# The second softmax's factor of a differential attention on GpSimd instead of VectorE, with other waits in its written order

## The chip, the core and the metric

The kernel runs on one core of one Trainium2 chip. The metric is device time in microseconds (us) of one execution, the median of three runs. The core's engines work side by side, each through its own queue in order: TensorE (PE, matmuls and transposes), VectorE (DVE), ScalarE (ACT), GpSimd (POOL) and SyncE (SP, which issues the DMA transfers). Semaphores hold an instruction until its inputs are there.

## What is computed

One layer of an encoder over 512 tokens of width 1024, all in float32: a norm, one input projection, three branches (pooling, differential attention, a gated recurrence), their gated sum, an output projection, and a SwiGLU block. The change touches the attention, four heads, 128 queries at a time. Of the reference:

```python
s = jnp.einsum('bqhcd,bkhcd->bhcqk', qblk, k) * scale
s = s - slopes[:, None, None, None] * dist
p = jax.nn.softmax(s, axis=-1)
a = (p[:, :, 0] - lam * p[:, :, 1]).astype(v.dtype)
return jnp.einsum('bhqk,bkhe->bqhe', a, v)
...
o = rms_norm(o, gain) * (1.0 - lambda_init)
```

Each head has two softmaxes (c = 0 and 1). With e0, e1 the exponentials and z0, z1 their row sums, the kernel makes e0 + co * e1 with co = -lam * z0 / z1, which is z0 times the wanted difference; the head's norm brings 1/z0 in later.

## The kernel before

The program is one long list of TensorE work in an order written by hand. `Pipe.run` (L45) takes several generators, called streams here, and resumes the first whose time has come: `mm` and `transpose` add an assumed duration to a clock of its own, `yield ("w", t)` lets a stream sit out t of that clock, and `yield ("e", name, t)` makes it wait for a marked event and t more. `mm` and `transpose` keep TensorE's instructions in just that order (`keep_in_program_order`). No such yield becomes an instruction; it only decides what stands between two pieces of one stream. On the other engines a scheduler in the compiler orders the instructions.

In the attention stage run together: `att_head(h)` for four heads, `pool_windows()` (running sums for the pooling branch, VectorE alone) and `jobs.stream` (the projections: per job eight 128x512 matmuls each of `hT_hi` with `whi`, `hT_lo` with `whi`, `hT_hi` with `wlo`; the branch projections read `y_arena` instead). Each job's weights arrive by DMA in `raw`; ScalarE rounds them into `whi` (L183) and VectorE subtracts the rest into `wlo` (L184). Weight buffers are three deep, so a later `wlo` waits for TensorE to finish an earlier job.

`att_front_job` makes a head's operands: q from one job, k from the next. Of k, ScalarE makes two rounded copies (L1019, L1020), VectorE the rest `l` (L1021) and ScalarE a copy of that (L1023), for c = 0 and then for c = 1.

`att_head(h)`, four query blocks i of 128 rows each:

- `scores(i)`: for c = 0, 1 two 128x512 matmuls into a bank of `rc` (q with k, q with l); VectorE adds the distance penalty and takes the row's minimum (L1056, `s` and `mx`); ScalarE takes the exponential and its row sum into `zz` (L1058, an activation and a short read of its accumulator). Then on VectorE: reciprocals of both row sums (L1062, `rr`), the factor `co` (L1064), and the combination over 128x512 (L1066, `s`).
- `turn(i)`: TensorE transposes that `s` in four pieces into `tp` (L98); ScalarE rounds it into `aT_hi` (L1075), VectorE subtracts into `aT_lo` (L1076).
- after four blocks, twelve matmuls `rc<-aT,va` with the values, then `head_norm`: squares on ScalarE, their sums by matmuls with `onesD`, three small VectorE operations `mo` (L663 to L665) that bring in 1/z0, a power of -0.5 on GpSimd (L140, `rso`), one more product on VectorE (L667) and transposes of `rso`.

Blocks are named head.block below, 0.0 to 3.3. A block's combination must be done when its transposes come up in TensorE's queue, or all matmuls behind them wait. Two lines of the loop set the distance:

```python
yield ("w", 1.8 + (0.7 if i == 0 else 0.0))   # L1080, then scores(i + 1)
yield ("w", 1.6 + (1.0 if i + h == 0 else 0.0))   # L1085, then turn(i)
```

Of the kernel before, what the change touches and what calls it, by code (L numbers as in the profile page):

```python
# [11 lines left out]
F32 = mybir.dt.float32  # L12
# [3 lines left out]
ALU = mybir.AluOpType  # L16
PSUM = bass.MemoryType.PSUM

P = 128
S = 512  # L20
D = 1024
NB = S // P
# [16 lines left out]
class Pipe:  # L39
# [8 lines left out]
    def mark(self, name):  # L48
        self.events[name] = self.t
# [27 lines left out]
def encoder_kernel(ctx: ExitStack, tc: tile.TileContext, x, norm1_g, w_in, pool_w, pool_scale,  # L77
# [3 lines left out]
    nc = tc.nc  # L81
# [3 lines left out]
    def pool(name, bufs=1, **kw):  # L85
        return tc.tile_pool(name=name, bufs=bufs, **kw)


    def mm(out_, lhsT, rhs, start, stop, chain=False):
        i = nc.tensor.matmul(out_, lhsT=lhsT, rhs=rhs, start=start, stop=stop, skip_group_check=chain)  # L90
        tc.keep_in_program_order(i)
        n = 1
        for d in rhs.shape[1:]:
            n *= d
        pipe.t += max(0.107, n * 0.0004167 + 0.002) if rhs.dtype == F32R else max(0.216, n * 0.001667 + 0.004)

    def transpose(out_, in_, idn):
        tc.keep_in_program_order(nc.tensor.transpose(out_, in_, idn))  # L98
        pipe.t += 0.108
# [8 lines left out]
    const = ctx.enter_context(pool("const"))  # L108
    wraw = ctx.enter_context(pool("wraw", 2))
    wsp = ctx.enter_context(pool("wsp", 3))  # L110
    small = ctx.enter_context(pool("small", 5))
    psum = ctx.enter_context(pool("psum", 3, space=PSUM))

    def bank(name, shape=(P, 512)):
        return psum.tile(list(shape), F32, name=name, bufs=2 if name == "tp" else 3)
# [11 lines left out]
    nc.vector.memset(onesD, 1.0 / P)  # L127
    mhalf = const.tile([P, 8], F32, name="mhalf")
    nc.vector.memset(mhalf, -0.5)
    masks = const.tile([P, len(LEVELS), P], U8, name="masks")  # L130
    vcol = const.tile([P, 14], F32, name="vcol")
    gain_a = const.tile([P, 1], F32, name="gain_a")
    lb = const.tile([P, 8], F32, name="lb")
    om = const.tile([P, 8], F32, name="om")
    nlam = const.tile([P, 1], F32, name="nlam")
# [3 lines left out]
    def pow_mhalf(dst, src):  # L139
        return nc.gpsimd.tensor_tensor(out=dst, in0=src, in1=mhalf[:, :src.shape[1]], op=ALU.pow).ins  # L140

    def rsqrt_eps(dst, mean):

        ms = small.tile([P, 8], F32, name="ms")[:, :mean.shape[1]]
        eng = nc.vector if mean.space == PSUM else nc.gpsimd
        eng.tensor_scalar(out=ms, in0=mean, scalar1=1.0, scalar2=EPS, op0=ALU.mult, op1=ALU.add)
        return pow_mhalf(dst, ms)
# [431 lines left out]
    ps = bank("mm")  # L579
# [67 lines left out]
    def head_norm(o_ps, tmp, gain, r0=None, bufs=2):  # L647


        og = tmp.tile([P, S], F32, name="og", bufs=bufs)  # L650
        sq = tmp.tile([P, S], F32, name="sqo", bufs=bufs)
        nc.scalar.activation(out=sq, in_=o_ps, func=AF.Square)
        nc.scalar.activation(out=og, in_=o_ps, func=AF.Copy, scale=gain)
        yield ("w", 1.3)
        sp = bank("tp")
        for b in range(NB):
            mm(sp[:, b:b + 1], sq[:, b * P:(b + 1) * P], onesD, True, True)
        r = small.tile([P, NB], F32, name="rso")
        if r0 is None:
            rsqrt_eps(r, sp[:, 0:NB])  # L660
        else:
            m = small.tile([P, NB], F32, name="mo")
            nc.vector.tensor_tensor(out=m, in0=sp[:, 0:NB], in1=r0, op=ALU.mult)  # L663
            nc.vector.tensor_tensor(out=m, in0=m, in1=r0, op=ALU.mult)
            nc.vector.tensor_scalar(out=m, in0=m, scalar1=EPS, scalar2=None, op0=ALU.add)  # L665
            pow_mhalf(r, m)
            nc.vector.tensor_tensor(out=r, in0=r, in1=r0, op=ALU.mult)  # L667
        yield ("w", 3.55)
        rb = bank("tp")
        for b in range(NB):  # L670
            transpose(rb[:, b * P:(b + 1) * P], r[:, b:b + 1].to_broadcast([P, P]), ident)
        return og, rb
# [359 lines left out]
    def att_head(h):  # L1032
        if h:
            yield ("e", f"QK{h - 1}", 0.0)
        if h > 1:
            yield ("e", f"AN{h - 2}", 0.0)
        yield ("e", f"AF{h}", 6.0)
        t = att.pop(h)
        at, (vh, vl), aT, y_attn = ATT["at"], ATT["v"], ATT["aT"], ATT["y"]
        strip = ATT["strip"].tile([P, 896], F32, name="strip")  # L1040
        nc.sync.dma_start(out=strip, in_=c_dist[h])
        zz = at.tile([P, NB, 2], F32, name="zz")
        rr = at.tile([P, NB, 2], F32, name="rr")
        probs = {}

        def scores(i):
            bs = slice(i * P, (i + 1) * P)
            mx = small.tile([P, 2], F32, name="mx")
            ex = []
            for c in range(2):  # L1050
                ps = bank("rc")
                mm(ps, t[f"q{c}"][:, bs], t[f"k{c}"], True, False)
                mm(ps, t[f"q{c}"][:, bs], t[f"l{c}"], False, True)
                s = at.tile([P, S], F32, name=f"s{c}")

                nc.vector.tensor_tensor_reduce(out=s, in0=strip[:, 384 - P * i:896 - P * i], in1=ps, scale=1.0,  # L1056
                                               scalar=3.0e38, op0=ALU.add, op1=ALU.min, accum_out=mx[:, c:c + 1])
                nc.scalar.activation(out=s, in_=s, func=AF.Exp, scale=-1.0, bias=mx[:, c:c + 1],  # L1058
                                     accum_out=zz[:, i, c:c + 1])
                ex.append(s)  # L1060

            nc.vector.reciprocal(out=rr[:, i, :], in_=zz[:, i, :])  # L1062
            co = small.tile([P, 1], F32, name="co")
            nc.vector.scalar_tensor_tensor(out=co, in0=zz[:, i, 0:1], scalar=nlam, in1=rr[:, i, 1:2],  # L1064
                                           op0=ALU.mult, op1=ALU.mult)
            nc.vector.scalar_tensor_tensor(out=ex[0], in0=ex[1], scalar=co, in1=ex[0], op0=ALU.mult, op1=ALU.add)  # L1066
            probs[i] = ex[0]

        def turn(i):
            bs = slice(i * P, (i + 1) * P)  # L1070
            p = probs.pop(i)
            pt = bank("tp", (P, NB, P))
            for k in range(NB):
                transpose(pt[:, k, :], p[:, k * P:(k + 1) * P], ident)
            nc.scalar.copy(out=aT[0][:, :, bs], in_=pt)  # L1075
            nc.vector.tensor_tensor(out=aT[1][:, :, bs], in0=pt, in1=aT[0][:, :, bs].bitcast(F32), op=ALU.subtract)  # L1076

        scores(0)
        for i in range(NB):
            yield ("w", 1.8 + (0.7 if i == 0 else 0.0))  # L1080
            if i + 1 < NB:
                scores(i + 1)
            else:
                mark(f"QK{h}")
            yield ("w", 1.6 + (1.0 if i + h == 0 else 0.0))  # L1085
            if h and i == 0:
                yield ("e", f"PV{h - 1}", 0.0)
            turn(i)
        mark(f"T{h}")
        yield ("e", "VA", 1.5)  # L1090
        yield ("w", 1.5)
        ps = bank("rc")
        es = slice(h * P, (h + 1) * P)
        terms = [(vh, aT[0]), (vl, aT[0]), (vh, aT[1])]
        for i, (a, r) in enumerate(terms):
            for k in range(NB):
                mm(ps, a[:, k, es], r[:, k, :], i == 0 and k == 0, i == 2 and k == NB - 1)
            yield
        mark(f"PV{h}")
        og, rbp = yield from head_norm(ps, at, gain_a, rr[:, :, 0], 1)  # L1100
        mark(f"AN{h}")
        nc.vector.tensor_tensor(out=og, in0=og, in1=rbp, op=ALU.mult)
        nc.scalar.copy(out=y_attn[0][:, h, :], in_=og)
        nc.vector.tensor_tensor(out=y_attn[1][:, h, :], in0=og, in1=y_attn[0][:, h, :].bitcast(F32),
                                op=ALU.subtract)
# [725 lines left out]
```

## Time and profile before

| what | value |
|---|---|
| median of three runs | 886.88 us (886.32 to 886.91) |
| the profiled execution's own time | 886.27 us |
| its span, first to last instruction | 884.5 us |
| TensorE busy (matmuls) | 867.9 us, 98% |
| VectorE busy | 664.5 us, 75% |
| ScalarE busy | 448.4 us, 51% |
| GpSimd busy | 18.7 us, 2%, 35 instructions |
| attention stage | about 215 to 345 us of the span |

A timeline row has the start in us from the span's start, the duration in us, engine, line, operation, the tile written and the tiles read, the count, and in brackets the idle time before it with what ended it. A matmul row's duration runs into the next one's start, since matmuls overlap; the step from start to start is what TensorE spends. In a row of the waits stand: who waited, for whom, us in total, times, the longest.

### The profile page before, as it was taken

How to read it: one execution, taken by the hardware profiler on the slowest of the kernel's cores; microseconds unless marked ns; L12 is line 12 of the kernel's file. 1: busy time of each engine (PE TensorE's matmuls, PEld its weight loads, DVE VectorE, ACT ScalarE, POOL GpSimd, SP SyncE). 2: the span in 40 equal slices, each digit the busy share in tenths (PEclk: the TensorE clock that was granted, in tenths of full speed). 3: DMA queues.
4: the chain of work that ended last, by engine and by line, in shares of the span. 5: the costliest groups of instructions: out<-in, count | busy, mean ns of one | idle time of the engine just before them, and what ended most of it. 6: DMA issues, size and time to landing. Idle time of an engine off the chain costs nothing.

```text
span 884.5 us, 14079 instructions
## 1 busy us (share of the span) xinstructions
PE 867.9 (98%) x5713; PEld 786.7 (89%) x5713; DVE 664.5 (75%) x1005; ACT 448.4 (51%) x718; POOL 18.7 (2%) x35
## 2 busy tenths in 40 slices
PE   8999999999999989999999999999999999999996
PEld 7989988888998867899999898999999999988885
DVE  6788664844857876987877555998888888747996
ACT  6544343434746743553455334755555655533463
POOL 1000000000000000000000001000000000000001
PEclk9999999999999999999999999999999999999999
DMA  8330113024123311334331770153443443355002
GB/s 243 96 120 24 49 48 116 27 73 141 49 88 94 94 61 49 96 96 137 101 97 48 262 191 1 49 143 96 125 115 96 123 118 97 119 190 189 2 1 96
DMA packets 115693, 87.53 MB, mean 99 GB/s; under 512 B 3862, under 2 KB 104748, under 8 KB 115628
## 3 DMA queue, kind: packets, MB, share of 16 engines
q1 hardware_dynamic: 115036, 85.57, 32.0%
q8 instruction: 45, 0.74, 0.3%
q10 hardware_dynamic: 592, 1.05, 0.3%
q14 instruction: 20, 0.16, 0.1%
HBM read 84.52 MB, written 2.10 MB: 98 GB/s over the span
## 4 chain that ended last, share of the span: by engine, by line
PE 87%; DVE 7%; DMA 2%; issue 1%; ACT 1%; POOL 0%; SPq 0%; POOLq 0%; DVEq 0%; ACTq 0%
PE mm L90 58%; PE rc L90 26%; PE tp L90 2%; PE tp L98 1%; DVE wlo L184 1%; DMA raw<-in_w_out_dram 1%; DMA raw<-in_w_in_dram 1%; DVE hid L354 1%; DVE flo L354 1%; DMA xin<-in_x_dram 0%; DVE s L1066 0%; DVE win L1159 0%; DVE hrow L481 0%; DVE h_lo L498 0%; PE rc L98 0%
## 5 line engine op out<-in xcount | busy, mean ns | idle before, releaser
L183 ACT CAST whi<-raw 128x1024 fp32r<-128x1024 f32 (+1 forms) x134 | 127.5, 958 | 138.4 <-PE mm L90 88.6
L184 DVE TENSOR_TENSOR wlo<-raw,whi 128x1024 fp32r<-128x1024 f32 (+1 forms) x134 | 147.6, 1106 | 58.2 <-ACT whi L183 35.5
L90 PE MATMUL mm<-hT_hi,whi 128*128 128x512 f32 (+1 forms) x344 | 82.1, 371 | 0.0
L90 PE MATMUL mm<-hT_hi,wlo 128*128 128x512 f32 (+1 forms) x344 | 81.7, 370 | 0.2 <-DVE wlo L184 0.2
L90 PE MATMUL mm<-hT_lo,whi 128*128 128x512 f32 (+1 forms) x344 | 81.5, 372 | 0.0
L302 DVE TENSOR_TENSOR slo<-sums,shi 128x1024 fp32r<-128x1024 f32 x58 | 70.5, 1218 | 0.2 <-ACT shi L300 0.2
L90 PEld LDWEIGHTS mm<-hT_lo,whi 128*128 128x128 f32 x344 | 60.0, 191 | 9.9
L90 PEld LDWEIGHTS mm<-hT_hi,whi 128*128 128x128 f32 x344 | 58.9, 189 | 9.9 <-ACT hT_hi L494 0.4
L90 PEld LDWEIGHTS mm<-hT_hi,wlo 128*128 128x128 f32 x344 | 58.5, 188 | 9.5 <-DVE wlo L184 0.4
L300 ACT CAST shi<-sums 128x1024 fp32r<-128x1024 f32 x58 | 61.0, 1053 | 4.1 <-DVE sums L264 3.7
L261 DVE TENSOR_TENSOR sums<-raw 128x1024 f32<-128x1024 f32 x29 | 35.4, 1219 | 1.7 <-DMA raw<-in_w_in_dram 1.6
L90 PE MATMUL mm<-y_arena,whi 128*128 128x512 f32 x128 | 32.8, 394 | 0.0
L90 PE MATMUL mm<-whi,y_arena 128*128 128x256 f32 (+1 forms) x192 | 31.9, 315 | 0.4 <-ACT whi L183 0.2
L914 DVE TENSOR_TENSOR kq<-kq,pyr 128x256 f32<-128x256 f32 x48 | 18.2, 421 | 18.2 <-PE rc L90 18.2
L90 PE MATMUL rc<-kq,kc 128*128 128x128 f32 x224 | 31.6, 284 | 0.0
L90 PEld LDWEIGHTS rc<-kq,kc 128*128 128x128 f32 x224 | 30.1, 191 | 1.5
L1058 ACT ACTIVATE s<-s,mx 128x512 f32<-128x512 f32 x32 | 23.0, 720 | 16.7 <-DVE mx L1056 16.5
L90 PEld LDWEIGHTS mm<-whi,y_arena 128*128 128x128 f32 x192 | 27.4, 188 | 3.5 <-ACT whi L183 1.0
L883 ACT COPY kc<-kq 128x512 f32<-128x512 f32 x28 | 18.6, 666 | 20.2 <-PE rc L90 12.6
L90 PEld LDWEIGHTS mm<-y_arena,whi 128*128 128x128 f32 x128 | 23.7, 188 | 5.1
L1346 DVE TENSOR_TENSOR g<-mm,g 128x256 f32<-128x256 f32 x21 | 8.9, 424 | 23.7 <-PE mm L90 23.7
L90 PE MATMUL mm<-fhi,slo 128*128 128x256 f32 x168 | 26.1, 277 | 0.5 <-DVE slo L302 0.5
(383 smaller groups left out, 2031.5 us busy)
## 6 DMA issues: line engine op xcount, KB each, us to landing
raw<-in_w_in_dram SPq DMA_DIRECT2D x44, 512.0 KB, 4.2
raw<-in_w_ffn_in_dram SPq DMA_DIRECT2D x44, 512.0 KB, 5.3
raw<-in_w_in_dram SPq DMA_DIRECT2D x8, 1024.0 KB, 5.2
raw<-in_w_ffn_out_dram SPq DMA_DIRECT2D x7, 1024.0 KB, 5.0
raw<-in_w_out_dram SPq DMA_DIRECT2D x4, 1024.0 KB, 11.1
xin<-in_x_dram SPq DMA_DIRECT2D x4, 512.0 KB, 4.6
raw<-in_w_up_rec_dram SPq DMA_DIRECT2D x2, 1024.0 KB, 6.4
raw<-in_w_up_pool_dram SPq DMA_DIRECT2D x2, 1024.0 KB, 5.1
```

The source lines that it names most:

```text
L90: i = nc.tensor.matmul(out_, lhsT=lhsT, rhs=rhs, start=start, stop=stop, skip_group_check=chain)
L98: tc.keep_in_program_order(nc.tensor.transpose(out_, in_, idn))
L183: nc.scalar.copy(out=hi, in_=view)
L184: LAST["wlo"] = nc.vector.tensor_tensor(out=lo, in0=view, in1=hi.bitcast(F32), op=ALU.subtract).ins
L261: nc.vector.tensor_tensor(out=strided(sums, 0, [[2 * half, 2], [1, half]]), in0=strided(self.raw, 0, [[3 * half, 2], [1, half]]), in1=stri ...
L300: nc.scalar.copy(out=hi, in_=view)
L302: on_dve = nc.vector.tensor_tensor(out=lo, in0=view, in1=hi.bitcast(F32), op=ALU.subtract).ins
L354: last[0] = form(**kw).ins
L883: nc.scalar.copy(out=strided(kc, 0, [[2 * n, S // (2 * n)], [n, 2], [1, n]]), in_=strided(kq, 2 * S, [[2 * n, S // (2 * n)], [S + n, 2], [ ...
L914: nc.vector.tensor_tensor(out=xv, in0=xv, in1=tv, op=ALU.mult)
L1058: nc.scalar.activation(out=s, in_=s, func=AF.Exp, scale=-1.0, bias=mx[:, c:c + 1], accum_out=zz[:, i, c:c + 1])
L1346: on_dve = nc.vector.tensor_tensor(out=c["g"], in0=c["x"], in1=c["g"], op=ALU.add).ins
```

## The change

The factor leaves VectorE. Per block GpSimd makes `zn` = z0 * -lam, `co` = z1 to the power of -1 (with a column of -1.0, `minus1`), and `co` = `co` * `zn`; the combination on VectorE is as it was, now waiting for GpSimd. The reciprocal of z0 is taken once per head for all four blocks, behind the last `turn`. The yield ahead of `scores(i + 1)` goes from 1.8 to 1.6, the one ahead of `turn(i)` from 1.6 to 2.4. One memset of 128x1 is new at the start. Lines move down by two or three.

```diff
+    minus1 = const.tile([P, 1], F32, name="minus1")
+    nc.vector.memset(minus1, -1.0)
...
-        rr = at.tile([P, NB, 2], F32, name="rr")
+        rr = at.tile([P, NB], F32, name="rr")
...
-            nc.vector.reciprocal(out=rr[:, i, :], in_=zz[:, i, :])
-            co = small.tile([P, 1], F32, name="co")
-            nc.vector.scalar_tensor_tensor(out=co, in0=zz[:, i, 0:1], scalar=nlam, in1=rr[:, i, 1:2],
-                                           op0=ALU.mult, op1=ALU.mult)
+            zn, co = (small.tile([P, 1], F32, name=n) for n in ("zn", "co"))
+            nc.gpsimd.tensor_tensor(out=zn, in0=zz[:, i, 0:1], in1=nlam, op=ALU.mult)
+            nc.gpsimd.tensor_tensor(out=co, in0=zz[:, i, 1:2], in1=minus1, op=ALU.pow)
+            nc.gpsimd.tensor_tensor(out=co, in0=co, in1=zn, op=ALU.mult)
             nc.vector.scalar_tensor_tensor(out=ex[0], in0=ex[1], scalar=co, in1=ex[0], op0=ALU.mult, op1=ALU.add)
...
         for i in range(NB):
-            yield ("w", 1.8 + (0.7 if i == 0 else 0.0))
+            yield ("w", 1.6 + (0.7 if i == 0 else 0.0))
             if i + 1 < NB:
                 scores(i + 1)
             else:
                 mark(f"QK{h}")
-            yield ("w", 1.6 + (1.0 if i + h == 0 else 0.0))
+            yield ("w", 2.4 + (1.0 if i + h == 0 else 0.0))
             if h and i == 0:
                 yield ("e", f"PV{h - 1}", 0.0)
             turn(i)
         mark(f"T{h}")
+        nc.vector.reciprocal(out=rr, in_=zz[:, :, 0])
...
-        og, rbp = yield from head_norm(ps, at, gain_a, rr[:, :, 0], 1)
+        og, rbp = yield from head_norm(ps, at, gain_a, rr, 1)
```

TensorE, from the last score matmul of block 3.3 to its transposes; `s_3066` and `s_3103` are block 3.2, `s_3125` and `s_3168` block 3.3. Before:

```order
L90 MATMUL rc<-l_2760,q_2756 128x512
L90 MATMUL mm<-y_arena,whi 128x512 x2
L90 MATMUL mm<-y_arena,wlo 128x512 x4
L90 MATMUL mm<-y_arena,whi 128x512 x2
L98 MATMUL tp<-ident,s_3066 128x128 x4
L90 MATMUL mm<-y_arena,whi 128x512 x6
L90 MATMUL mm<-y_arena,wlo 128x512 x4
L90 MATMUL mm<-hT_hi,whi 128x512 x8
L98 MATMUL tp<-ident,s_3125 128x128 x4
```

And of the change:

```order
L90 MATMUL rc<-l_2765,q_2761 128x512
L90 MATMUL mm<-y_arena,whi 128x512 x8
L90 MATMUL mm<-y_arena,wlo 128x512 x4
L98 MATMUL tp<-ident,s_3103 128x128 x4
L90 MATMUL mm<-hT_hi,whi 128x512 x8
L90 MATMUL mm<-hT_lo,whi 128x512 x8
L90 MATMUL mm<-hT_hi,wlo 128x512 x4
L98 MATMUL tp<-ident,s_3168 128x128 x4
```

Between the last score matmul and the transposes stood 26 other matmuls of 128x512, now 32, and one block's transposes both times.

VectorE at the same place, behind the two minima of block 3.3. Before, from the first row behind them; behind these twelve follow `co`, `pwlo`, the `gate` combination of L1168 and then the combination of block 3.3:

```order
L1181 TENSOR_TENSOR dlo<-gate,dhi 128x512
L756 TENSOR_TENSOR merged<-mm,gate 128x512
L1159 TENSOR_TENSOR win<-win 128x525
L1076 TENSOR_TENSOR aT_lo<-tp,aT_hi 128x4x128
L1130 MEMSET gate 128x8
L1131 MEMSET gate 128x8
L1062 RECIPROCAL rr<-zz 128x2
L1130 MEMSET gate 128x8
L1131 MEMSET gate 128x8
L756 TENSOR_TENSOR merged<-mm,gate 128x512
L1166 SCALAR_TENSOR_TENSOR win<-win,rcnt 128x2x8
L184 TENSOR_TENSOR wlo<-raw,whi 128x1024
```

Of the change, from the second memset behind the minima up to the combination:

```order
L1134 MEMSET gate 128x8
L1184 TENSOR_TENSOR dlo<-gate,dhi 128x512
L1169 SCALAR_TENSOR_TENSOR win<-win,rcnt 128x2x8
L1092 RECIPROCAL rr<-zz 128x4
L758 TENSOR_TENSOR merged<-mm,gate 128x512
L1133 MEMSET gate 128x8
L1134 MEMSET gate 128x8
L1171 SCALAR_TENSOR_TENSOR gate<-win,gate 128x512
L186 TENSOR_TENSOR wlo<-raw,whi 128x1024
L1178 TENSOR_TENSOR pwlo<-pw,pwhi 128x512
L1078 TENSOR_TENSOR aT_lo<-tp,aT_hi 128x4x128
L1068 SCALAR_TENSOR_TENSOR s_3168<-s_3174,co,s_3168 128x512
```

One `merged`, one `win` of 128x525 and `co` no longer stand between the minima and the combination; the first two now stand ahead of the minima.

TensorE at the first scores of head 2, from the end of the job that makes its k (`mm<-hT_hi,wlo`). Before:

```order
L90 MATMUL mm<-hT_hi,wlo 128x512 x2
L90 MATMUL mm<-y_arena,whi 128x512 x8
L90 MATMUL mm<-y_arena,wlo 128x512 x4
L90 MATMUL mm<-y_arena,whi 128x512 x4
L98 MATMUL tp<-ident,s_2632 128x128 x4
L90 MATMUL mm<-y_arena,whi 128x512 x4
L90 MATMUL mm<-y_arena,wlo 128x512 x4
L90 MATMUL rc<-aT_hi,va_hi 128x512 x4
L90 MATMUL rc<-aT_hi,va_lo 128x512 x4
L90 MATMUL rc<-aT_lo,va_hi 128x512 x4
L90 MATMUL rc<-k_2506,q_2504 128x512
```

And of the change:

```order
L90 MATMUL mm<-hT_hi,wlo 128x512 x8
L90 MATMUL mm<-y_arena,whi 128x512 x4
L98 MATMUL tp<-ident,s_2588 128x128 x4
L90 MATMUL mm<-y_arena,whi 128x512 x4
L90 MATMUL mm<-y_arena,wlo 128x512 x4
L90 MATMUL mm<-y_arena,whi 128x512 x8
L90 MATMUL mm<-y_arena,wlo 128x512 x4
L98 MATMUL tp<-ident,s_2651 128x128 x4
L90 MATMUL rc<-k_2521,q_2519 128x512
L90 MATMUL rc<-l_2523,q_2519 128x512
L90 MATMUL rc<-k_2522,q_2520 128x512
L90 MATMUL rc<-l_2524,q_2520 128x512
```

The first scores of head 2 now stand ahead of head 1's product with the values, and 24 matmuls of 128x512 and two blocks' transposes behind the end of the k job, where 36 matmuls and one block's transposes stood.

## The prediction

> **What bounds the kernel now.** First the page: busy time per engine, then the waits of TensorE.
>
> ```profile
> PE 867.9 (98%) x5713; PEld 786.7 (89%) x5713; DVE 664.5 (75%) x1005; ACT 448.4 (51%) x718; POOL 18.7 (2%) x35
> ```
>
> ```profile
> PE tp L98 <- DVE s L1066: 2.8, 1, 2.8
> PE tp L98 <- DVE rr L1062: 1.0, 1, 1.0
> PE tp L98 <- DVE rso L667: 0.6, 1, 0.6
> ```
>
> TensorE is busy in 98% of the span, and its list of matmuls is the same before and after. So VectorE time taken off is worth nothing in itself: the time moves only where TensorE stands still or runs at a lower clock. These three waits, all in the attention stage, are most of what a change there can win. Now TensorE's timeline at them, with one undisturbed job as the measure.
>
> ```profile
> 340.69 1.99 PE L90 MATMUL mm<-hT_lo,whi 128*128 128x512 f32 x8
> 342.52 0.61 PE L90 MATMUL mm<-hT_hi,wlo 128*128 128x512 f32 x2
> 343.69 0.62 PE L98 MATMUL tp<-ident,rso 128*128 128x128 f32 x4 [0.56 <-DVE rso L667]
> ...
> 276.42 1.08 PE L90 MATMUL mm<-y_arena,wlo 128*128 128x512 f32 x4
> 277.65 1.20 PE L90 MATMUL rc<-aT_hi,va_hi 128*128 128x512 f32 x4
> ...
> 309.30 0.95 PE L90 MATMUL tp<-onesD,sqo 128*128 128x1 f32 x8
> 311.25 0.63 PE L98 MATMUL tp<-ident,s 128*128 128x128 f32 x4 [1.01 <-DVE rr L1062]
> ...
> 320.18 0.39 PE L90 MATMUL rc<-l,q 128*128 128x512 f32 x1
> ...
> 324.98 1.98 PE L90 MATMUL mm<-hT_hi,whi 128*128 128x512 f32 x8
> 329.75 1.09 PE L98 MATMUL tp<-ident,s 128*128 128x128 f32 x4 [2.79 <-DVE s L1066]
> 330.49 3.06 PE L90 MATMUL mm<-hT_lo,whi 128*128 128x512 f32 x8
> 333.39 1.08 PE L90 MATMUL rc<-aT_hi,va_hi 128*128 128x512 f32 x4
> ```
>
> Eight matmuls step 342.52 - 340.69 = 1.83 us, 0.229 each; I count losses from start to start. Block 3.3: 329.75 - 324.98 - 1.83 = 2.94. Block 3.0: the eight passes of `onesD` step about 0.81 elsewhere in this stage, so 311.25 - 309.30 - 0.81 = 1.14. The norm of head 3: 343.69 - 342.52 - 2 x 0.229 = 0.71. The product with the values of head 1: 277.65 - 276.42 - 4 x 0.229 = 0.31. Behind the longest wait the work itself is slow: the eight matmuls at 330.49 take 2.90 instead of 1.83, the transposes 0.74 instead of 0.35, 1.46 lost. The windows say why.
>
> ```profile
> 328.00:330.00 2.00, 0.25 (x2) 0.28 (x3) 1.60 (x3) 0.00 (x0) 0.00 (x0) 0.79 0.00 0
> 330.00:332.00 2.00, 2.00 (x8) 1.71 (x8) 0.51 (x1) 0.59 (x1) 0.00 (x0) 0.50 0.00 0
> ```
>
> The granted clock (third number from the end) falls to 0.50 in the 2.8 us wait. Together 2.94 + 1.14 + 0.71 + 0.31 + 1.46 = **6.56 us** are there to be won, no more.
>
> **Part 1: the factor on GpSimd.** What goes from VectorE and what the new operations cost:
>
> ```profile
> 287.08 0.17 DVE L1062 RECIPROCAL rr<-zz 128x2 f32<-128x2 f32 x1 [0.91 <-ACT s L1058]
> 287.28 0.22 DVE L1064 SCALAR_TENSOR_TENSOR co<-zz,nlam,rr 128x1 f32<-128x1 f32 x1
> 287.54 0.75 DVE L1066 SCALAR_TENSOR_TENSOR s<-s,co,s 128x512 f32<-128x512 f32 x1
> ```
>
> ```profile
> L140 POOL TENSOR_TENSOR rstd<-ms,mhalf x8: 550/554/562, 6.0 to 553.2; 128x1 f32<-128x1 f32 x8
> L146 POOL TENSOR_SCALAR ms<-ss x8: 192/192/419, 5.7 to 552.9; 128x1 f32<-128x1 f32 x8
> ```
>
> From the second row sum (the releaser in the first row, 0.03 ahead of it) to the combination VectorE needs 287.54 - 287.08 + 0.03 = 0.49 us. On GpSimd `zn` needs only z0 and is early. Then comes a power of 128x1, 0.55 by the row above (exponent -0.5 there, -1 here), and a product of 128x1, for which the nearest row is `ms`, 0.19. With some 0.08 at each of three handovers that is 0.98 us, 0.5 longer. VectorE loses 16 x (0.17 + 0.22 + gaps of 0.05) = 7.0 us and gains 4 reciprocals of 0.17 per run; both lie beside TensorE's work. What counts is whether the combination, first in VectorE's queue while GpSimd works, holds what stands behind it: at most 0.5 us per block if nothing else is late.
>
> GpSimd can be held itself:
>
> ```profile
> 283.96 0.75 DVE L1066 SCALAR_TENSOR_TENSOR s<-s,co,s 128x512 f32<-128x512 f32 x1
> 284.18 1.40 POOL L140 TENSOR_TENSOR rso<-mo,mhalf 128x4 f32<-128x4 f32 x1 [20.22 <-DVE mo L665]
> ...
> 200.06 1.01 POOL L140 TENSOR_TENSOR rso<-ms,mhalf 128x4 f32<-128x4 f32 x1 [52.81 <-DVE ms L146]
> 200.92 1.23 DVE L184 TENSOR_TENSOR wlo<-raw,whi 128x1024 fp32r<-128x1024 f32 x1 [0.94 <-PE mm L90]
> ```
>
> A power that began during a combination took 1.40 instead of the 1.01 of the third row, longer by about what was left of that combination. The other way round, a `wlo` that began 0.15 before a power ended took its usual 1.23. So a GpSimd operation may wait out a `wlo` (1.2 us), but then VectorE is at work, not idle; the cost left over is again about one power and one product. I take 0.5 us of need per block, bounds 0 and 0.5 + 1.2. The Trainium skill, page "SBUF — State Buffer", section "Who interferes with whom", speaks against the change: a VectorE instruction with two inputs in SBUF and a GpSimd instruction that reads SBUF lock each other out, and whichever comes second waits for the whole of the first. By that rule VectorE's combinations and `wlo` would wait for powers too, and up to 16 x 0.93 = 15 us of VectorE time would be added, an estimate from the rows above; the trace agrees for GpSimd waiting (1.40) and not for VectorE waiting (1.23).
>
> **Part 2: the distances.** The order rows above give TensorE's work from the start of a block's last score matmul to its transposes; transposes of an earlier block cost about 0.46 with the step behind them.
>
> Block 3.3: before 27 x 0.229 + 0.46 = 6.6 us, after 33 x 0.229 + 0.46 = 8.0.
>
> ```profile
> 318.31 1.23 DVE L184 TENSOR_TENSOR wlo<-raw,whi 128x1024 fp32r<-128x1024 f32 x1
> ...
> 321.94 0.68 DVE L1056 CUSTOM_DVE_ANT_0 s<-strip,rc 128x512 f32<-128x512 f32 x1
> ...
> 323.76 0.68 DVE L756 TENSOR_TENSOR merged<-mm,gate 128x512 f32<-128x512 f32 x1
> 324.36 0.70 DVE L1159 TENSOR_TENSOR win<-win 128x525 f32<-128x525 f32 x1
> ...
> 328.86 0.75 DVE L1066 SCALAR_TENSOR_TENSOR s<-s,co,s 128x512 f32<-128x512 f32 x1
> ```
>
> The need before was 329.60 - 320.18 = 9.4: VectorE has no idle time before any row from the `wlo` to the combination, and eleven pieces of other work lay between the minima and the combination. Now one `merged` and one `win` (0.6 each by their steps) and `co` (0.2) are gone from there, 1.4 less. Both stand ahead of the minima instead, but the first `wlo` row, which starts as the matmuls before it end, now has 12 matmuls and a block's transposes between it and the scores instead of 6, 1.8 us more, against 1.2 us of added rows: the minima come 0.6 sooner. Need 9.4 - 1.4 - 0.6 = 7.4 to 9.4, against 8.0: a stall of 0 to 1.4; I take 0.3, near the lower end, because the rows removed are counted and only the start is unsure.
>
> Block 3.0:
>
> ```profile
> 304.43 0.39 PE L90 MATMUL rc<-l,q 128*128 128x512 f32 x1
> ```
>
> ```profile
> 310.36 0.74 DVE L1066 SCALAR_TENSOR_TENSOR s<-s,co,s 128x512 f32<-128x512 f32 x1
> ```
>
> Need 310.36 + 0.74 - 304.43 = 6.7; offered 5.7 before, and after 27 matmuls and `onesD`, 27 x 0.229 + 0.81 = 7.0. The wait of 1.14 goes. All other blocks gain 0.7 to 1.9 us of distance against 0.5 of need, but for 1.0 and 1.1, which had over 12 us of slack; the tightest of the rest, 1.3, had its combination done 0.5 us early and gets 1.3 more.
>
> The norm of head 3 now has 12 matmuls instead of 18 between `onesD` and its transposes, 2.7 us for a chain that took 4.8; but two `win` additions, the `gate` combination and a `wlo`, which stood among or ahead of its small steps, now come before or after all of them, and what is left (0.5 on VectorE, 1.0 to 1.6 on GpSimd, 0.2) fits. 0.71 goes; bounds 0 and 0.71.
>
> **What is new and late.** Head 2's scores come earlier against the job that makes its k: 24 matmuls and two transposes, 6.4 us to the first, 7.1 to the last that needs the second `l`. The two chains of this kind in the trace:
>
> ```profile
> 271.38 2.01 PE L90 MATMUL mm<-y_arena,whi 128*128 128x512 f32 x8
> ...
> 297.34 0.62 PE L90 MATMUL mm<-hT_hi,whi 128*128 128x512 f32 x2
> ```
>
> ```profile
> 278.56 0.62 ACT L1023 CAST l<-l 64x512 fp32r<-64x512 f32 x1
> ...
> 303.14 0.62 ACT L1023 CAST l<-l 64x512 fp32r<-64x512 f32 x1
> ```
>
> The jobs end where these matmul rows begin; the second `l` was ready 279.18 - 271.38 = 7.8 and 303.76 - 297.34 = 6.4 us later. Against 7.1 that is a stall of 0.7 or none; I take 0.4. For head 3 the distance stays 7.1.
>
> **The sum.** 886.27 (the profiled execution; span 884.5 and 1.8 around it) - 6.56 + 0.3 + 0.4 = 880.4. The median of the runs is 0.6 above that execution: **881.0 us**. The extra memset and the 48 small GpSimd instructions have idle queues.
>
> **Rivals.**
> 1. The last block still waits. VectorE's burst is shifted, not shortened: need near 9.4, stall 1.4, and the clock falls again, 1.46. That gives 881.0 - 0.3 + 2.9 = 883.6. For it: VectorE had no pause there. Against: three rows are gone. A wait of 1.0 us at block 3.0 cost no clock.
> 2. The win is given back behind the stage. VectorE is fully busy there:
>
> ```profile
> 350.00:360.00 10.00, 10.00 (x46) 8.24 (x45) 10.00 (x12) 6.64 (x9) 0.00 (x0) 1.00 0.00 0
> ```
>
> TensorE arrives 6 us sooner, VectorE owes the same sums, and a later `wlo` is late: up to 6.56 back, 886.9. The change would then do what it says and not show. Against: VectorE waits for TensorE itself before that stretch:
>
> ```profile
> 338.22 1.22 DVE L184 TENSOR_TENSOR wlo<-raw,whi 128x1024 fp32r<-128x1024 f32 x1 [6.04 <-PE mm L90]
> ```
>
> 3. Slower. In the burst of blocks 3.1 to 3.3 each combination waits for a power held by a `wlo` (1.2) and a product held by a `win` (0.6): 0.98 + 1.2 + 0.6 - 0.49 = 2.3 us more per block, and since VectorE has no slack there they add up: 3 x 2.3 = 6.9, less the 0.5 that block 3.3 has over, 6.4, with 1.46 of clock and 0.4 for head 2: 886.88 - 6.56 + 8.3 = 888.6, and with 0.7 at the norm 889.3. It turns slower above 3x - 0.5 + 1.46 + 0.4 + 0.7 = 6.56, x = 1.5 us per block. Against: while GpSimd is held, VectorE is doing the very work.
>
> **How the numbers follow.** Forecast 0.62, rival 1 0.18, rival 2 0.10, rival 3 0.10. About 0.2% (1.8 us) is what a measurement here can tell from no change. The forecast and rival 1 lie below 885.1: faster 0.80; same 0.10, slower 0.10. The lower end is everything won and 0.3 of spread, 880.0; the upper takes in rival 1 with stalls of 0.7 and 0.7 more at the norm and head 2, 885.0.
>
> **What would show it.** Right: no wait of TensorE over 0.3 us on block 3.0, 3.3 or the norm, clock 1.00 throughout 320 to 340, a short wait at head 2's first scores. Each combination starts about 1 us after its second row sum where nothing else delays it. Wrong: transposes that wait for a combination which itself waited for `co` (rival 3), 0.50 of clock in the stage (rival 1), or new waits for `wlo` after 345 us (rival 2).

## The result and the profile after

The changed kernel takes **896.59 us** (median of four runs, 896.18 to 897.01), against 886.89 before in the same comparison: a ratio of 1.011 (95% interval 1.0092 to 1.0127). It is slower by 1.1%; the forecast was 881.0, faster. The profiled execution took 897.01 us, its span is 895.2. In the experiments one run of e5 (2247.61 us) and one of e8 (1307.41) were slow and are left out of the medians.

First the page of after, busy time per engine, and the top of TensorE's waits (who, for whom, us in total, times, the longest).

```profile
PE 882.5 (99%) x5713; PEld 795.5 (89%) x5713; DVE 661.6 (74%) x978; ACT 449.4 (50%) x718; POOL 37.0 (4%) x83
```

```profile
PE mm L90 <- POOL ident masks.py:199: 1.3, 1, 1.3
PE rc L90 <- ACT l L1025: 1.2, 1, 1.2
PE tp L98 <- DVE hrow L483: 0.6, 1, 0.6
```

The three waits that the change was expected to remove (2.8, 1.0 and 0.6 us before) are gone from the list, and the one new wait is the expected one, for the second `l` of head 2. Yet TensorE, with the same 5713 matmuls, is **busy 14.6 us longer** (867.9 before). The timeline of the attention stage shows both at once: no bracket, so no idle time, at blocks 3.0 (316.65) and 3.3 (333.78) or at the norm (344.39).

```profile
316.65 0.60 PE L98 MATMUL tp<-ident,s 128*128 128x128 f32 x4
...
330.97 2.04 PE L90 MATMUL mm<-hT_lo,whi 128*128 128x512 f32 x8
332.85 1.09 PE L90 MATMUL mm<-hT_hi,wlo 128*128 128x512 f32 x4
333.78 0.60 PE L98 MATMUL tp<-ident,s 128*128 128x128 f32 x4
...
344.39 0.60 PE L98 MATMUL tp<-ident,rso 128*128 128x128 f32 x4
```

```profile
320.00:330.00 10.00, 10.00 (x51) 8.22 (x49) 9.55 (x25) 6.19 (x13) 1.78 (x4) 1.00 0.39 131
330.00:340.00 10.00, 10.00 (x47) 8.11 (x46) 7.89 (x12) 4.22 (x8) 1.30 (x2) 1.00 0.19 59
```

The granted clock is 1.00 in both windows, where it fell to 0.50 before (the prediction's window 330 to 332). But the eight matmuls at 330.97 step 332.85 - 330.97 = 1.88 us, 0.235 each; the undisturbed job of before stepped 1.83. That is no effect of the attention stage. Here are the same matmuls long after it, before and then after:

```profile
421.34 0.62 PE L90 MATMUL mm<-hT_hi,whi 128*128 128x256 f32 x4
421.80 0.62 PE L90 MATMUL mm<-hT_lo,whi 128*128 128x256 f32 x4
...
424.06 0.62 PE L90 MATMUL mm<-ghi,shi 128*128 128x256 f32 x4
424.52 0.62 PE L90 MATMUL mm<-glo,shi 128*128 128x256 f32 x4
```

```profile
422.37 0.64 PE L90 MATMUL mm<-hT_hi,whi 128*128 128x256 f32 x4
422.85 0.64 PE L90 MATMUL mm<-hT_lo,whi 128*128 128x256 f32 x4
...
425.24 0.62 PE L90 MATMUL mm<-ghi,shi 128*128 128x256 f32 x4
425.69 0.62 PE L90 MATMUL mm<-glo,shi 128*128 128x256 f32 x4
```

Four matmuls that read `whi` step 0.48 us after and 0.46 before; four that read `shi` step 0.45 and 0.46, the same. So certain pairs of operands are slower, all over the kernel. Grouped by the tiles they read, with the duration's minimum, median and maximum in ns, before and then after:

```profile
L90 PE MATMUL mm<-fhi,shi x168: 276/276/384, 565.1 to 761.4; 128*128 128x256 f32 x168
L90 PE MATMUL mm<-fhi,whi x84: 276/276/385, 570.9 to 764.1; 128*128 128x256 f32 x84
L90 PE MATMUL mm<-hT_lo,whi x344: 276/389/776, 13.5 to 482.8; 128*128 128x512 f32 x132, 128*128 128x256 f32 x40
```

```profile
L90 PE MATMUL mm<-fhi,shi x168: 275/276/386, 568.8 to 769.6; 128*128 128x256 f32 x168
L90 PE MATMUL mm<-fhi,whi x84: 277/282/388, 574.4 to 772.3; 128*128 128x256 f32 x84
L90 PE MATMUL mm<-hT_lo,whi x344: 277/394/530, 13.8 to 485.2; 128*128 128x512 f32 x132, 128*128 128x256 f32 x40
```

`fhi` with `whi` takes 282 ns instead of 276, `hT_lo` with `whi` 394 instead of 389; `fhi` with `shi` is unchanged. The start times in the same lines show the loss growing along the program: the last `fhi,shi` starts 8.2 us later than before, the first 3.7 later.

What differs between the two programs there? Not the instructions and not the clock, but where the tiles stand. `minus1` takes 32 bytes of each partition in pool `const`, `zn` 5 x 32 = 160 in pool `small`, and all that is allocated behind them moves. The compiled programs give these start addresses (bytes within a partition; of `whi` the first of the three buffers in which most parts stand, the others 4352 = 17 x 256 further):

| tile | before | after | moved |
|---|---|---|---|
| `whi` | 34592 | 34624 | 32 |
| `hT_hi` | 61984 | 62176 | 192 |
| `fhi` | 195808 | 196000 | 192 |
| `shi`, the buffer that `fhi` meets | 179232 | 179424 | 192 |
| `y_arena`, from the other end | 212512 | 212512 | 0 |

So `whi` against `hT` and `fhi` has another distance; `fhi` against `shi` has not (179232 - 195808 and 179424 - 196000 are the same). A pair is named here as its rows name it: first the operand that streams through, then the weights.

### The profile page after: what moved, and what is told of

It reads as the page before. It is cut to its first block, busy times and chain, and to the rows that moved or that the text cites. A ratio compares the mean times of both kernels' runs of the same rounds, so it can differ in the third digit from the quotient of the medians.

```text
span 895.2 us, 14111 instructions
## 1 busy us (share of the span) xinstructions
PE 882.5 (99%) x5713; PEld 795.5 (89%) x5713; DVE 661.6 (74%) x978; ACT 449.4 (50%) x718; POOL 37.0 (4%) x83
## 3 DMA queue, kind: packets, MB, share of 16 engines
q10 hardware_dynamic: 592, 1.05, 0.3%
## 4 chain that ended last, share of the span: by engine, by line
PE 86%; issue 7%; DMA 3%; DVE 2%; ACT 1%; POOL 0%; SPq 0%; POOLq 0%; ACTq 0%; DVEq 0%
PE mm L90 56%; PE rc L90 26%; PE tp L90 2%; DMA raw<-in_w_in_dram 2%; PE tp L98 1%; DMA raw<-in_w_out_dram 1%; DVE wlo L186 1%; DMA xin<-in_x_dram 0%; ACT whi L185 0%; ACT s L1060 0%; POOL rso L142 0%; PE rc L98 0%; DVE hrow L483 0%; DVE slo L304 0%; ACT hrow L477 0%
## 5 line engine op out<-in xcount | busy, mean ns | idle before, releaser
L90 PE MATMUL mm<-hT_hi,whi 128*128 128x512 f32 (+1 forms) x344 | 83.9, 375 | 0.0
```

## Experiments

The kernels in each of the three rounds below were compared with their own runs of the kernel before (886.73, 886.21 and 886.78 us; the last kernel with 887.12). "Step" is the time from one matmul's start to the next one's of the same pair, the mean over undisturbed steps in the trace; a table of all steps stands behind the last experiment.

### First round: is it the places of the tiles?

**e1_after_old_places**: the whole change, its two small tiles put where nothing moves.

```diff
-    minus1 = const.tile([P, 1], F32, name="minus1")
+    minus1 = warm
...
-            zn, co = (small.tile([P, 1], F32, name=n) for n in ("zn", "co"))
+            zc = small.tile([P, 2], F32, name="co")
+            zn, co = zc[:, 0:1], zc[:, 1:2]
```

> The whole change, with its two new small tiles put into storage that exists already, so that every tile has the SBUF address it had before. Theory P (place: the two tiles shift all tiles behind them, and matmuls read slower there): TensorE's steps are those of before (0.227 us per 128x512 matmul, not 0.233), the waits of before in the attention stage stay gone, the new one at head 2's scores (1.2 us) stays: 886.9 - 6.6 + 1.2 = 881.5 us, 880.5 to 882.5. Rival G (the GpSimd work or the new order slows TensorE): about 896.6, as the change itself, steps 0.233.

Measured: 881.61 us (880.29 to 882.46), ratio 0.9937 (0.9922 to 0.9952). With both tiles out of the way the change gains nearly what its waits promised; the places cost the 15 us between this kernel and the change. Summed over all matmuls from start to start, the traces of the change and of e1 differ by 14.6 us: 11.1 of it lies in the pairs of `hT`, `h`, `f`, `g` with `whi` or `wlo`, and 0.0 in the pairs of `h`, `f`, `g` with `shi` or `slo`, whose distance is the same. The one new wait is still there, shorter:

```profile
PE rc L90 <- ACT l L1025: 0.8, 1, 0.8
```

**e2_before_new_places**: the kernel before, with two unused tiles of the same sizes, so that its own tiles stand as in the change.

```diff
+    spare = const.tile([P, 1], F32, name="spare")
+    nc.vector.memset(spare, -1.0)
...
+            small.tile([P, 1], F32, name="zn")
```

> The kernel before with only the two tiles added and not used (32 bytes per partition early, 160 more in the pool of small tiles), so that every tile has the address it has in the change. Theory P: the slower steps without the change, 886.9 + 15 = 902, 899 to 904. Rival G: 886.9, within 0.5.

Measured: 901.77 us, ratio 1.0163 (1.0147 to 1.0178). Two tiles that nothing reads cost 15 us. Neither GpSimd nor the new order is needed for the loss.

**e3_before_plus32** and **e4_before_plus160** have one of the two tiles each: e3 the one of 32 bytes in `const`, which moves everything but `y_arena`; e4 the 160 bytes in `small`, which leave `whi` and `y_arena` in place and move `hT`, `h`, `f`, `g` and `s`.

> The kernel before with the early 32 bytes alone: weights and activations shift alike and start at 0 modulo 64 bytes, where they started at 32; only the y arenas at the other end of SBUF stay. Theory P1 (a start at 0 modulo 64 is slow): nearly all matmuls slower, over 900. Theory P2 (the distance between the two operands counts, fast at a multiple of 64): only matmuls of a y arena with weights slow, some 3 us: 888 to 891.

> The kernel before with the 160 bytes alone: weight parts stay at 32 modulo 64, activations behind them go to 0 modulo 64. P1: slow wherever the operand that moved is the one that counts; if the weights of the projections (the parts whi and wlo) alone count, 887. P2: slow for all pairs of a weight part with an activation, about as in the change, 899 to 904.

Measured: e3 888.1 us, ratio 1.0012 (1.0002 to 1.0022); e4 899.61 us, ratio 1.0143 (1.0126 to 1.016). In e3 only the pairs with `y_arena` step slower (230.7 to 233.8 ns for 512 elements), in e4 only the pairs of `hT`, `h`, `f`, `g` with `whi` or `wlo` (228.5 to 233.9 and 113.5 to 118.6). A move that keeps the distance costs nearly nothing (the most is `ghi` with `shi` in e4, from 113.3 to 115.2), one that changes it does. Up to here a remainder by 64 of the distance was taken to decide.

### Second round: which distances, and what the change's parts are worth

**e5_after_padded**: the change with its own tiles, both padded to multiples of 64 bytes.

```diff
-    minus1 = const.tile([P, 1], F32, name="minus1")
+    minus1 = const.tile([P, 16], F32, name="minus1")[:, 0:1]
...
+            zn = small.tile([P, 16], F32, name="zn")[:, 0:1]
+            co = small.tile([P, 1], F32, name="co")
```

> The change as it stands, with its own two new tiles, but both padded, so that all addresses move by multiples of 64 bytes: whi and wlo by 64, hT, the h, f, g and s tiles by 384, y_arena stays. The addresses are new, all distances keep their remainder by 64 (some change it by 128). Theory P2 (only an operands' distance of 32 by 64 is slow): steps of 227 ns for hT_hi with whi and 113 ns for 256 elements, time as in e1_after_old_places, 880.5 to 882.5 us. Rival: any move of the tiles, or a distance that is no multiple of 128, is slow: 227 to 233 and 113 to 118, time 893 to 897 us.

Measured: 898.39 us, ratio 1.0137 (1.0113 to 1.016). The expectation of 881.5 failed, and the remainder by 64 with it: `hT` to `whi` had gone from 0 to 192 by 256, `f` to `whi` from 64 to 0 by 128. Worse, pairs whose distance had not changed at all slowed too:

```profile
423.13 0.64 PE L90 MATMUL mm<-ghi,shi 128*128 128x256 f32 x4
423.60 0.64 PE L90 MATMUL mm<-glo,shi 128*128 128x256 f32 x4
```

Four of them step 0.47 us here, against 0.46 before; the mean step of `ghi` with `shi` went from 113.3 to 117.8 ns.

**e6_waits_alone**: the kernel before with the two yields alone (1.6 and 2.4), the factor on VectorE, no new tile.

> The kernel before with only the two yields of the change (1.6 and 2.4), the factor as before on VectorE, all addresses as before. Theory D (the new distances alone take the waits away, the factor on GpSimd adds nothing to that): no wait of TensorE at blocks 3.0 and 3.3 over 0.5 us, 881 to 882.5 us. Rival F (VectorE's lighter load is needed at block 3.3): VectorE keeps the factor's operations (16 x 0.44 us), block 3.3 still waits 0.7 to 1.4 us with the clock at 0.50 behind it, 883 to 885 us.

Measured: 880.97 us, ratio 0.9944 (0.9931 to 0.9957), just under theory D's range; F fell. Block 3.3's transposes come 329.28 - 321.19 = 8.1 us behind its last score matmul, and its combination is done at 329.13, 7.9 behind; there is no wait at 3.0, 3.3 or the norm. Head 2's first scores wait 0.6 us for `l` here too.

```profile
321.19 0.39 PE L90 MATMUL rc<-l,q 128*128 128x512 f32 x1
...
329.28 0.63 PE L98 MATMUL tp<-ident,s 128*128 128x128 f32 x4
```

```profile
328.38 0.75 DVE L1066 SCALAR_TENSOR_TENSOR s<-s,co,s 128x512 f32<-128x512 f32 x1
```

**e7_gpsimd_alone**: as e1, but with the yields of before (1.8 and 1.6).

> The factor on GpSimd with the yields of before (1.8 and 1.6), all addresses as before. Theory D: block 3.3 stands 6.4 us behind its scores for a need of 7.4 to 9.4, so the waits at block 3.3 (1 to 3 us) and at block 3.0 stay, and the need per block is 0.5 us longer, so blocks 0.3, 1.3 and 2.3 may wait too: 885.5 to 888.5 us. Rival F (the relief of VectorE brings the gain): the wait at block 3.3 is under 0.7 us, 881 to 883.5 us.

Measured: 882.55 us, ratio 0.996 (0.9947 to 0.9973). Theory D fell here and F held: with the old distance block 3.3 waits 0.39 us only (block 3.0 still 1.05), although a block's factor takes longer on GpSimd. VectorE's timeline says why. First before, what stood ahead of the combination of 328.86; then e7, with TensorE's row of the block.

```profile
326.39 1.22 DVE L184 TENSOR_TENSOR wlo<-raw,whi 128x1024 fp32r<-128x1024 f32 x1
...
327.65 0.68 DVE L1175 TENSOR_TENSOR pwlo<-pw,pwhi 128x512 fp32r<-128x512 f32 x1
328.26 0.68 DVE L1168 SCALAR_TENSOR_TENSOR gate<-win,gate 128x512 f32<-128x512 f32 x1
```

```profile
320.17 0.39 PE L90 MATMUL rc<-l,q 128*128 128x512 f32 x1
...
327.33 0.63 PE L98 MATMUL tp<-ident,s 128*128 128x128 f32 x4 [0.39 <-DVE s L1069]
```

```profile
326.43 0.75 DVE L1069 SCALAR_TENSOR_TENSOR s<-s,co,s 128x512 f32<-128x512 f32 x1
327.10 1.22 DVE L186 TENSOR_TENSOR wlo<-raw,whi 128x1024 fp32r<-128x1024 f32 x1
```

Without the reciprocal and the product in VectorE's queue the compiler's order has the combination ahead of the `wlo`: the need is 326.43 + 0.75 - 320.17 = 7.0 us instead of 9.4. So either part of the change takes most of block 3.3's stall away by itself, and together they gain no more than the yields alone.

**e8_after_later_head2**: e1 with the first scores of head 2 later in the written order.

```diff
-        yield ("e", f"AF{h}", 6.0)
+        yield ("e", f"AF{h}", 6.8 if h == 2 else 6.0)
```

> e1_after_old_places with the first scores of head 2 set 0.8 later in the written order: four more matmuls of 128x512 (0.91 us) between the job that makes its k and its scores. If the one new wait there (0.8 us for the second l) is nothing but that distance, it goes and no other comes: 0.8 us less than e1_after_old_places, 880.3 to 881.2 us. If the wait moves on to the transposes of block 2.0, which get 0.9 us less distance (5.9 for 6.8): as e1_after_old_places, 881.2 to 882.4 us.

Measured: 880.38 us, ratio 0.9938 (0.9924 to 0.9952). The wait for `l` is gone from the list and none came in its place. It is the fastest version here, though its interval overlaps those of e1 and e6.

### Third round: the remainder that counts

**e9_after_padded128**, **e10_before_gap64** and **e11_before_all64** use the kernel's own helper `pad` (L101), which reserves bytes in a pool.

```diff
 e9, the change:
+    pad(const, 96, "cpad")
+    pad(small, 96, "spad")
 e10, before:
+    pad(small, 64, "spad")
 e11, before:
+    pad(const, 64, "cpad")
```

> The change as it stands with its own tiles, padded once more: whi and wlo move by 128 bytes, everything behind the small pool by 384, so hT and the h, f, g and s tiles stand exactly where they stood in e5_after_padded, and only whi and wlo stand 64 bytes further. Theory M (the distance from the operand that streams to the weights that are loaded next counts by its remainder by 128: 64 is fast for 256 elements, 0 for 512, others slow): all distances as before, steps of 227 and 113 ns, 880.5 to 882.5 us. Rival A (the absolute places count): the f, g and h tiles with the s tiles step 117 to 118 ns as in e5_after_padded, 884.5 to 887 us, or more if whi is slow too.

> The kernel before with 64 bytes of padding behind the small pool: hT and the h, f, g and s tiles move by 64, whi, wlo and y_arena stay. Theory M: every distance to whi and wlo changes its remainder by 128, so those pairs are slow (120 for 256 elements, 229 to 230 for 512), f, g, h with the s tiles stay at 113, y_arena pairs stay: 893 to 898 us. If only the remainder by 64 counted: 886 to 888 us. Rival A: f, g, h with the s tiles leave 113 as well.

> The kernel before with 64 bytes of padding in the const pool: every tile on the left side moves by 64, only y_arena stays. hT and the h, f, g and s tiles stand where they stand in e10_before_gap64. Theory M: all distances but those to y_arena are as before, so only the y_arena pairs are slow, 887 to 890 us. Rival A (absolute places count): steps of hT, h, f or g leave 227 and 113 ns, 892 us or more.

Measured: e9 882.87 us, ratio 0.9953 (0.9941 to 0.9966); e10 902.28 us, ratio 1.017 (1.0154 to 1.0185); e11 888.65 us, ratio 1.0017 (1.0008 to 1.0026). The groups of e9, then of e10:

```profile
L90 PE MATMUL mm<-fhi,shi x168: 276/276/386, 561.2 to 757.5; 128*128 128x256 f32 x168
L90 PE MATMUL mm<-fhi,whi x84: 276/276/385, 567.0 to 760.2; 128*128 128x256 f32 x84
L90 PE MATMUL mm<-hT_lo,whi x344: 276/389/540, 13.8 to 478.4; 128*128 128x512 f32 x132, 128*128 128x256 f32 x40
```

```profile
L90 PE MATMUL mm<-fhi,shi x168: 275/281/387, 571.5 to 776.2; 128*128 128x256 f32 x168
L90 PE MATMUL mm<-fhi,whi x84: 278/283/384, 577.3 to 779.1; 128*128 128x256 f32 x84
L90 PE MATMUL mm<-hT_lo,whi x344: 278/392/632, 13.4 to 488.0; 128*128 128x512 f32 x132, 128*128 128x256 f32 x40
```

In e9 `f`, `h` and `s` stand exactly where they stood in e5, and all three pairs are as fast as before (`fhi` with `shi`, both at the places of e5, 113.4 ns against 117.4), so it isn't the absolute places; in e11 too a move of 64 without a change of distance left them alone. The change keeps its own tiles and is faster than before. e10 came out above the 893 to 898 us expected, because `fhi` with `shi` went to 281 ns as in e5 at an unchanged distance; that part of theory M failed. e9 is 0.4 us above the range expected: its pairs with `y_arena`, moved by 128, had gone from 230.7 to 233.0, which led to the last run.

**e12_before_gap128**: e10 with 128 bytes in place of 64.

> The kernel before with 128 bytes of padding behind the small pool: hT and the h, f, g and s tiles move by 128, whi, wlo and y_arena stay. In e9_after_padded128 the distances kept their remainder by 256 for all pairs but those with y_arena, whose distance changed by 128, and these went from 230.7 to 233.0 ns. Theory M (the remainder by 128 decides): hT with whi stays at 228 ns, f and h with whi at 113 to 114, 886 to 889 us. Rival M256 (the remainder by 256 decides): those pairs leave 228 and 113 ns, f and h with whi go to 117 to 120, 893 to 903 us.

Measured: 892.64 us, ratio 1.0061 (1.0042 to 1.008), between the two.

```profile
L90 PE MATMUL mm<-fhi,whi x84: 276/276/384, 575.4 to 768.7; 128*128 128x256 f32 x84
L90 PE MATMUL mm<-hT_lo,whi x344: 276/392/628, 13.8 to 487.3; 128*128 128x512 f32 x132, 128*128 128x256 f32 x40
```

Both theories were half right. Matmuls of 256 elements keep 276 ns, for them the remainder by 128 decides; those of 512 do not, for them it is the remainder by 256. All steps together, each with the remainder of its distance (weights' start less the streaming operand's start; "d" by 256 for 512 elements, by 128 for 256 elements; mean ns):

| kernel | us | `hT_hi,whi` 512 | `fhi,whi` 256 | `fhi,shi` 256, d 64 in all | `y_arena,whi` 512 (d of most) |
|---|---|---|---|---|---|
| before | 886.89 | d 0: 228.5 | d 64: 113.5 | 113.5 | d 0: 230.7 |
| e1 | 881.61 | d 0: 228.7 | d 64: 113.9 | 113.7 | d 0: 230.2 |
| e9 | 882.87 | d 0: 228.9 | d 64: 113.5 | 113.4 | d 128: 233.0 |
| e3 | 888.1 | d 0: 228.3 | d 64: 113.9 | 113.7 | d 32: 233.8 |
| e11 | 888.65 | d 0: 228.7 | d 64: 114.0 | 114.0 | d 64: 232.9 |
| e12 | 892.64 | d 128: 232.4 | d 64: 113.3 | 113.7 | d 0: 230.5 |
| after | 896.59 | d 96: 233.9 | d 32: 118.6 | 113.5 | d 32: 233.4 |
| e4 | 899.61 | d 96: 233.9 | d 32: 118.6 | 113.5 | d 0: 230.9 |
| e2 | 901.77 | d 96: 233.9 | d 32: 118.6 | 113.4 | d 32: 233.3 |
| e5 | 898.39 | d 192: 229.6 | d 0: 119.8 | 117.4 | d 64: 232.7 |
| e10 | 902.28 | d 192: 229.8 | d 0: 119.9 | 117.6 | d 0: 230.8 |

The last column is a mean over two distances, because some parts of `whi` start 64 bytes further into their buffer. Taken apart, before has 228.9 ns at 0 and 233.6 at 64, e9 has 232.9 at 128 and 233.3 at 192. So at 192 `y_arena` is slow where `hT` in e5 and e10 is nearly as fast as at 0: the remainder by 256 sorts the rows of each pair, but it is not the whole rule.

## Why the prediction was wrong

**The step that failed** is the first one: "its list of matmuls is the same before and after", and from it "the time moves only where TensorE stands still or runs at a lower clock". The list was the same, the clock was 1.00, and TensorE stood still less; the matmuls themselves took longer. With it failed the sentence that counted the new memset at nothing because of its idle queue: the instruction was free, the bytes of its tile and of `zn` were not. No rival covered this, so even the range missed; the 0.10 for slower was given for rival 3, which did not occur. The missing term is +15.0 us (e1 to after, 881.61 to 896.59; and e2 gives the same 15.0 on the kernel before). It could have been looked for: the kernel's code reserves 64 or 192 bytes by `pad` in seven places, L107 among them, which does nothing but move the tiles behind it, and the addresses can be read from the compiled program.

**The terms that were right.** The waits of blocks 3.0 and 3.3, of head 3's norm and the clock's fall: gone, as the rows of after show. With the places of before restored the change gains 5.1 us (886.73 to 881.61), where the sum said 5.9; 881.61 against a forecast of 881.0. That these are so near is partly luck: the 0.3 at block 3.3 did not come, and the wait at head 2 was 0.4 longer than forecast. Block 3.3 needed 332.43 + 0.74 - 325.63 = 7.5 us (forecast 7.4 to 9.4) with 8.15 on offer (8.0), so not even the 0.3 came.

```profile
325.63 0.40 PE L90 MATMUL rc<-l,q 128*128 128x512 f32 x1
```

```profile
332.43 0.74 DVE L1068 SCALAR_TENSOR_TENSOR s<-s,co,s 128x512 f32<-128x512 f32 x1
```

**The factor on GpSimd.** Two blocks of after, GpSimd first, then VectorE's combinations:

```profile
269.23 0.55 POOL L1066 TENSOR_TENSOR co<-zz,minus 128x1 f32<-128x1 f32 x1 [0.32 <-ACT s L1060]
269.85 0.19 POOL L1067 TENSOR_TENSOR co<-co,zn 128x1 f32<-128x1 f32 x1
...
276.15 0.97 POOL L1066 TENSOR_TENSOR co<-zz,minus 128x1 f32<-128x1 f32 x1 [0.52 <-ACT s L1060]
```

```profile
270.08 0.75 DVE L1068 SCALAR_TENSOR_TENSOR s<-s,co,s 128x512 f32<-128x512 f32 x1 [0.42 <-POOL co L1067]
277.42 0.75 DVE L1068 SCALAR_TENSOR_TENSOR s<-s,co,s 128x512 f32<-128x512 f32 x1 [0.71 <-POOL co L1067]
```

The prices of 0.55 and 0.19 were exact for most. Five of the 16 powers took 0.96 to 1.18 us instead, longer as the prediction feared. In seven blocks VectorE stood waiting for `co`, 5.6 us in all by the trace's groups, and none of it reached TensorE. VectorE was not held in turn. Here a `wlo` began 0.02 us into a power and took 1.24 us, where the median is 1.22 in both kernels; the product behind the power was held (0.69 instead of 0.19) until the `wlo` had ended:

```profile
321.93 0.55 POOL L1066 TENSOR_TENSOR co<-zz,minus 128x1 f32<-128x1 f32 x1 [0.52 <-ACT s L1060]
322.56 0.69 POOL L1067 TENSOR_TENSOR co<-co,zn 128x1 f32<-128x1 f32 x1
```

```profile
321.95 1.24 DVE L186 TENSOR_TENSOR wlo<-raw,whi 128x1024 fp32r<-128x1024 f32 x1 [0.45 <-ACT s L1060]
```

So the lock of the Trainium skill ("SBUF — State Buffer", "Who interferes with whom") was seen from GpSimd's side alone. Rivals 1 and 3 did not occur: no transposes waited for a combination. Rival 2's mechanism did not occur either, TensorE waits 0.6 us in all for `wlo` in e1 as before. But e1 does not keep its whole lead: followed matmul by matmul through the two profiled executions it is 5.45 us behind the attention stage and 3.86 at the end. The rest goes in slower steps around 503 to 525 us and 570 to 593, to which the last section comes back.

**A term that was mis-sized**: the wait at head 2's first scores, 0.4 in the forecast, 1.24 us measured.

```profile
274.56 1.10 PE L90 MATMUL mm<-y_arena,whi 128*128 128x512 f32 x4
...
283.13 0.50 PE L90 MATMUL rc<-l,q 128*128 128x512 f32 x1 [1.24 <-ACT l L1025]
```

```profile
282.46 0.62 ACT L1025 CAST l<-l 64x512 fp32r<-64x512 f32 x1
```

The job of k ended at 274.56, and the second `l` was there 283.08 - 274.56 = 8.5 us later, not 6.4 to 7.8. In e1 the wait was 0.8, and in e8, with four more matmuls of distance, it is gone.

**A reason that was only half right**: that the distances do the work and the factor on GpSimd is paid for. e6 bears out the first half. e7 shows that the factor on GpSimd alone would have brought a ratio of 0.996, since the compiler's order changed with it.

## What to carry to other kernels

When a change adds, removes or resizes any tile, even one of 4 bytes, compare the start addresses of TensorE's operands before and after, and keep the distance between streaming operand and weights as it was by padding (here up to multiples of 256 bytes, as e9 does for `whi` and `hT`). A kernel whose TensorE never waits can still lose over 1% in its steps, so look at the step of one undisturbed job beside the waits. Two remedies for one stall don't add up: test each alone before paying for both.

## What was not expected of the hardware

The step of a matmul depends on the distance of its operands' start addresses: for `hT_hi` with `whi`, 512 elements, 228.5 ns at a multiple of 256 bytes, 229.7 at 192, 232.4 at 128, 233.9 at 96; for `fhi` with `whi`, 256 elements, 113.5 ns at 64 by 128, 118.6 at 32 and 119.9 at 0. The Trainium skill ("SBUF — State Buffer", "Who interferes with whom") gives TensorE two read ports, one for the streaming operand and one for the weights, and calls them independent. By that the places would not matter; these runs show that they do, by nearly 6% of a step, and the measurement decides. That the two reads collide is a guess, which no run here shows directly.

Three things stay open. At a good distance a pair can still run slow: `fhi` with `shi` at 117.5 ns in e5 and e10, where the pairs around it were at a distance of 0. Even with all places the same the step can differ between the profiled executions: `whi` streaming against `y_arena` (256 elements, distance 64 in all) steps 113.8 ns before and 113.4 in e8, but 117.8 in e1 and 117.7 in e6, where this stretch costs about 0.7 us. This is where part of e1's lead went. Such matmuls may hold on to a slow rhythm from the ones ahead; that is a guess, which no run tried. Last, 228.5 may not be the least: distances between the multiples of 32 were not tried.
